# The end of the gate-row chain moved from VectorE to GpSimd and ScalarE, and its transposes six places later

## The chip, the cores and the metric

One core of a Trainium2 chip runs the whole kernel. Times are microseconds of device time for one execution; the figure for a kernel is the median of several runs. The engines are TensorE (PE in the profile), VectorE (DVE), ScalarE (ACT), GpSimd (POOL) and SyncE (SP). Each takes its own instructions in order and waits for the others by semaphores.

## The reference

Two decoder layers over 512 tokens of width 1024, in float32. Each layer projects its input once, runs two branches over four heads each, and merges them:

```python
p = x @ W_in                       # q|k|v|gate, mLSTM q|k|v|o|i|f, merge gates
y_A = P_A(swish(g) * HeadNorm(Retention(q, k, v)))
y_B = P_B(sigmoid(o) * HeadNorm(mLSTM(conv(q), conv(k), v, i, f)))
x = LN(alpha * x + W_out(sigmoid(gA) * y_A + sigmoid(gB) * y_B))
x = LN(alpha * x + SwiGLU(x))
```

The mLSTM branch needs, for each head, rows over the 512 tokens made from the two scalar gates i and f:

```python
log_f = log_sigmoid(f_pre)
b = cumsum(log_f)                  # in chunks
m = running maximum of (i - b)     # the stabiliser
# weights exp(...) of the scores and of the carried state use b, i - b and m
```

These rows are the gate-row chain. The change concerns its last three operations: -(b + m), a copy of that row to the place from which it is transposed, and -m.

## The kernel before, in words

**Tiles.** Every matrix product is done in three float32 matmuls: operands are split into a rounded high part and the rest, and high x high, high x low and low x high are summed in PSUM. Weights arrive in 512 KB tiles (`wraw`, SP's queue, five buffers); ScalarE casts the high part (`whi`, L201) and VectorE subtracts for the low part (`wlo`, `lo_of`, L133). This is done about four tiles ahead of the matmuls.

**Stages of a layer.** For each of two pairs of retention heads, p = 0 and 1: four feature blocks for q and k (L266 to L268), then a value block (`tok_units`, L357 to L359, four weight tiles times four token blocks of 128), then a gate block of the same form. After the first pair's q and k comes one block for the mLSTM's i and f (`feat_if`). Then follow the mLSTM heads, the merge, and the SwiGLU. A value block's four PSUM banks are evacuated by ScalarE (`rvh`, L714) and VectorE (`rvl`, L133); the gate block needs the same four banks.

**Order.** TensorE's and SP's instructions run in the order in which the code issues them. For the other engines a scheduler places the instructions of these stages; GpSimd, VectorE and ScalarE then run in that order.

**Places for side work.** `tok_units` and `feat_mms` call `slot()` after each group of matmuls. `slot()` takes one step of the first generator in the queue `side`: `scores` (3 steps; scores and weights of one head), `weighted` (5 steps; the state and four token blocks of weighted sums, L491 to L493), `head_norms`, `if_cols` (the transposes of the gate rows), and `rest(n)`, n steps that do nothing. A value or gate block has 16 places. After the gate block of each pair, `drain()` runs whatever is left in the queue, one step after another.

For p = 0 the queue at the value block is: `scores` of head 0, `rest(12)`, `if_cols`; behind it come `weighted` of head 0, `scores` of head 1, `rest(2)`, `weighted` of head 1.

**The gate-row chain.** `if_evac` (L632 on) makes the rows in the tile `rows`, four rows of heads in each of four slices r0 to r3, on VectorE and ScalarE, ending with a running maximum in two scans (L654). Its last three operations are at L658 to L660. Then r2 and the value `mp` are written to DRAM (`md`, L661 and L662, GpSimd's queue), from where they are read back over all partitions much later (`negm`, L740). `if_cols` transposes r3 on TensorE (L668), and copies the result to `cols` (L669) and `en` (L670), which the mLSTM stages use.

Of the kernel before, what the change touches and what calls it, by code (L numbers as in the profile page):

```python
# [13 lines left out]
ALU = mybir.AluOpType  # L14
# [90 lines left out]
def decoder_trunk(ctx: ExitStack, tc: tile.TileContext, wall, xT_in, x_in, pvec, lnp, rtab, out):  # L105
    nc = tc.nc
# [135 lines left out]
    side, slow = deque(), deque()  # L242
# [49 lines left out]
    def feat_split(xh, xl, evacs, between):  # L292

        ws = [take() for _ in evacs]
        pms = [main_bank() for _ in evacs]
        for n, (pm, w) in enumerate(zip(pms, ws)):
            feat_mms(pm, w, xh, xl, 0, S // 2, False)
            between(n)
        for pm, w, ev in zip(pms, ws, evacs):
            feat_mms(pm, w, xh, xl, S // 2, S)  # L300
            used()
            ev(pm)
# [277 lines left out]
    def input_sums(xh, xl, sh, sl):  # L580

        t1, t2 = slice(0, S // 2), slice(S // 2, S)
        for m in range(4):
            t = scratch([P, 2, S], "xs")
            for i in range(2):
                nc.gpsimd.tensor_tensor(out=t[:, i], in0=xh[:, m + 4 * i].bitcast(F32), in1=xl[:, m + 4 * i].bitcast(F32), op=ALU.add)
            yield
            f = scratch([P, 4, S // 2], "sf")
            a11, a12, a21, a22 = t[:, 0, t1], t[:, 1, t1], t[:, 0, t2], t[:, 1, t2]
            for i, a, b, op in ((0, a21, a22, ALU.subtract), (1, f[:, 0], a11, ALU.subtract),  # L590
                                (2, a11, a21, ALU.subtract), (3, f[:, 1], a12, ALU.add)):
                nc.vector.tensor_tensor(out=f[:, i], in0=a, in1=b, op=op)
            nc.scalar.copy(sh[:, :, m], f)
            lo_of(sl[:, :, m], f, sh[:, :, m])
            yield

    def rest(n):
        for _ in range(n):
            yield

    for l in range(L):
# [10 lines left out]
        def rot_evac(dst):  # L612
            def ev(pm):
                t = scratch([P, S], "rt")
                nc.vector.tensor_tensor(out=dst, in0=pm, in1=tab[:, 0], op=ALU.mult)
                nc.vector.tensor_tensor(out=t[0:64], in0=pm[64:128], in1=tab[0:64, 1], op=ALU.mult)
                nc.vector.tensor_tensor(out=t[64:128], in0=pm[0:64], in1=tab[64:128, 1], op=ALU.mult)
                nc.gpsimd.tensor_tensor(out=dst, in0=dst, in1=t, op=ALU.add)
            return ev
# [12 lines left out]
        def if_evac(pm):  # L632
            F = slice(32, 36)
            r0, r1, r2, r3 = (rows[:, i] for i in range(4))
            nc.gpsimd.memset(r3[0:32], 0.0)
            nc.vector.tensor_scalar(out=r0[0:36], in0=pm[0:36], scalar1=pv[0:36, C_BIF : C_BIF + 1], scalar2=None, op0=ALU.add)
            nc.vector.tensor_tensor(out=r0[0:36], in0=pm[64:100], in1=r0[0:36], op=ALU.add)
            nc.scalar.activation(r1[F], r0[F], AF.Abs)
            nc.scalar.activation(r1[F], r1[F], AF.Exp, scale=-1.0)
            nc.vector.tensor_scalar(out=r2[F], in0=r1[F], scalar1=1.0, scalar2=None, op0=ALU.add)  # L640
            nc.scalar.activation(r3[F], r2[F], AF.Ln)
            nc.vector.scalar_tensor_tensor(out=r1[F], in0=r2[F], scalar=-1.0, in1=r1[F], op0=ALU.add, op1=ALU.subtract)
            nc.scalar.activation(r2[F], r3[F], AF.Exp, scale=-1.0)
            nc.vector.tensor_tensor(out=r1[F], in0=r1[F], in1=r2[F], op=ALU.mult)
            nc.vector.tensor_tensor(out=r3[F], in0=r3[F], in1=r1[F], op=ALU.subtract)
            nc.vector.scalar_tensor_tensor(out=r1[F], in0=r0[F], scalar=0.0, in1=r3[F], op0=ALU.min, op1=ALU.subtract)
            for a in (slice(0, HC), slice(HC, S)):
                nc.vector.tensor_tensor_scan(out=r2[F, a], data0=r1[F, a], data1=r1[F, a], initial=0.0,
                                             op0=ALU.add, op1=ALU.min)
            nc.vector.tensor_copy(r1[0:4], r2[F])  # L650
            nc.vector.tensor_tensor(out=r3[0:4], in0=r0[0:4], in1=r1[0:4], op=ALU.subtract)
            mp = sm.tile([4, 1], F32, tag="mp", name="mp")
            for a, first in ((slice(0, HC), 0.0), (slice(HC, S), mp)):
                nc.vector.tensor_tensor_scan(out=r2[0:4, a], data0=r3[0:4, a], data1=r3[0:4, a], initial=first,  # L654
                                             op0=ALU.max, op1=ALU.max)
                if a.start == 0:
                    nc.vector.tensor_tensor(out=mp, in0=r1[0:4, HC - 1 : HC], in1=r2[0:4, HC - 1 : HC], op=ALU.add)
            nc.vector.scalar_tensor_tensor(out=r0[0:4], in0=r1[0:4], scalar=-1.0, in1=r2[0:4], op0=ALU.mult, op1=ALU.subtract)  # L658
            nc.vector.tensor_copy(r3[32:36], r0[0:4])
            nc.vector.tensor_scalar(out=r2[0:4], in0=r2[0:4], scalar1=-1.0, scalar2=None, op0=ALU.mult)  # L660
            nc.gpsimd.dma_start(md[:, :S], r2[0:4])  # L661
            nc.gpsimd.dma_start(md[:, S:], mp)  # L662

# [9 lines left out]
        for p in range(2):  # L673
            if p == 1:
                slow.append(input_sums(xh, xl, *xs))
            qk = reg.tile([P, 4, S], F32, tag="qk", name="rqk")
            rots = [rot_evac(qk[:, i]) for i in range(4)]
            if p == 0 and l > 0:
                feat_split(xh, xl, rots, between)
            elif p == 0:  # L680
                first_units(rots)
            else:
                for ev in rots:
                    feat(xh, xl, ev)
            if p == 0:
                feat_if(xh, xl, if_evac)
            boxes = [[None], [None]]

            def ret_weights(h):
                a = slice(h % 2 * HC, (h % 2 + 1) * HC)  # L690
                dec, qdec = tab[:, 2 + h // 2, a], tab[:, 4 + h // 2, a]

                def mult(o, a, c):
                    nc.vector.tensor_tensor(out=o[:, :HC], in0=a[:, :HC], in1=dec, op=ALU.mult)
                    nc.vector.tensor_tensor(out=o[:, HC:], in0=a[:, HC:W1], in1=dec[:, :P], op=ALU.mult)

                def key_weight():
                    return [pv[:, C_KW + 2 * h + j : C_KW + 2 * h + j + 1] for j in range(2)]

                def query_weight(o, q):  # L700
                    nc.vector.tensor_tensor(out=o, in0=q, in1=qdec, op=ALU.mult)

                return mult, key_weight, query_weight

            side.append(scores(qk, 0, boxes[0], *ret_weights(2 * p)))
            if p == 0:
                side.append(rest(12))
                side.append(if_cols())
            vh = reg.tile([P, NB, 2, DV], F32R, tag="vh", name="rvh")
            vl = reg.tile([P, NB, 2, DV], F32R, tag="vl", name="rvl")  # L710

            def v_evac(b, pm, vh=vh, vl=vl):
                src = pm.rearrange("p (h d) -> p h d", h=2)
                nc.scalar.copy(vh[:, b], src)  # L714
                lo_of(vl[:, b], src, vh[:, b])

            tok_units([main_bank() for _ in range(NB)], lambda k: xh[:, k], lambda k: xl[:, k], K8, True, True, v_evac)
            oo = reg.tile([P, 2, NB, DV], F32, tag="oo", name="roo")

            def o_done(hh, oo=oo):  # L720
                def done(i, pa):
                    nc.scalar.copy(oo[:, hh, i], pa[:, :DV])
                return done

            side.append(weighted(boxes[0], vh, vl, 0, DV, o_done(0)))
            side.append(scores(qk, 1, boxes[1], *ret_weights(2 * p + 1)))
            side.append(rest(2))
            side.append(weighted(boxes[1], vh, vl, 1, DV, o_done(1)))
            gt = reg.tile([P, NB, 2 * DV], F32, tag="gt", name="rgt")

            def g_evac(b, pm, gt=gt):
                nc.scalar.activation(gt[:, b], pm, AF.Silu)

            tok_units([main_bank() for _ in range(NB)], lambda k: xh[:, k], lambda k: xl[:, k], K8, True, True, g_evac)
            drain()
            gain = pv[:, C_RG : C_RG + 8]
            side.append(head_norms(oo, p, gt, gain, od[0]))
# [493 lines left out]
```

## Time and profile before

| | |
|---|---|
| median of 3 runs | 1776.57 us (1776.14 to 1777.71) |
| the profiled execution, its own time | 1777.92 us |
| its span, first to last instruction | 1776.2 us |
| granted TensorE clock, mean | 0.998 |
| TensorE busy | 1759.9 us, 99% |
| VectorE busy | 1312.9 us, 74% |
| ScalarE busy | 793.6 us, 45% |
| GpSimd busy | 433.3 us, 24% |
| the place of the change, layer 0 | 58 to 94 us |
| the place of the change, layer 1 | 937 to 973 us |

A row of a timeline has the start, the duration (both us), the engine, the line, the operation, what it writes and reads, the shape and the count; in brackets the idle time before it and what ended that. A row of waits has who waited for whom, the sum, the number and the longest. A row of groups has the number of instructions, busy us, the mean ns of one, and the idle time before.

### The profile page before, as it was taken

The page shows a single profiled execution, that of the slowest core. Times are in us where ns is not written, and L with a number is a line of the kernel's source. Part 1 is how long each engine was busy: PE and PEld are TensorE (multiplying, and loading weights), DVE is VectorE, ACT ScalarE, POOL GpSimd, SP SyncE. Part 2 cuts the span into 40 slices and gives each one's busy share as a digit, 9 for nine tenths or more (in the row PEclk, how much of TensorE's full clock was granted, in tenths as well). Part 3 has the DMA queues.
Part 4 walks back from the last instruction along what each step waited for, and adds up shares of the span by engine and source line. Part 5 has one row for each costly group of instructions (what it writes and reads, how often), then busy time and mean ns, then how long its engine had stood idle before and what let it go on. Part 6 is the DMA issues. An engine that isn't in the chain of part 4 may idle for free.

```text
span 1776.2 us, 27128 instructions
## 1 busy us (share of the span) xinstructions
PE 1759.9 (99%) x10904; PEld 1586.3 (89%) x10904; DVE 1312.9 (74%) x1726; ACT 793.6 (45%) x1148; POOL 433.3 (24%) x321
## 2 busy tenths in 40 slices
PE   9999999999999999999999999999999999999997
PEld 7888898998889999988898898989988899999886
DVE  6676878795559999963476968787845699998534
ACT  4445555663226444451244455556533254445310
POOL 2141110231001555520121311113300115555200
PEclk9999999999999999999999999999999999999999
DMA  7232422346333323363242323313553223333521
GB/s 250 86 105 72 143 72 96 106 137 239 96 111 110 105 96 108 107 213 95 83 166 89 110 88 106 119 60 108 200 180 119 95 95 108 111 116 114 186 69 48
DMA packets 74878, 209.48 MB, mean 118 GB/s; under 512 B 6616, under 2 KB 8536, under 8 KB 73728
## 3 DMA queue, kind: packets, MB, share of 16 engines
q1 hardware_dynamic: 64912, 168.32, 29.6%
q0 software_dynamic: 9840, 39.43, 6.3%
q8 instruction: 86, 1.41, 0.3%
q14 instruction: 40, 0.33, 0.1%
HBM read 190.93 MB, written 16.79 MB: 117 GB/s over the span
## 4 chain that ended last, share of the span: by engine, by line
PE 97%; DVE 1%; ACT 0%; issue 0%; DMA 0%; SPq 0%; DVEq 0%
PE pm L324 31%; PE pm L357 9%; PE pm L359 9%; PE pm L358 9%; PE pm L266 6%; PE pm L268 6%; PE pm L267 6%; PE pa L324 5%; PE pa L358 3%; PE pa L357 3%; PE pa L359 3%; PE pa L491 1%; PE pa L492 1%; PE pa L493 1%; PE pa L547 1%; PE pa L465 1%
## 5 line engine op out<-in xcount | busy, mean ns | idle before, releaser
L133 DVE TENSOR_TENSOR wlo<-wraw,whi 128x1024 fp32r<-128x1024 f32 (+2 forms) x416 | 599.6, 1453 | 203.1 <-ACT whi L201 200.5
L201 ACT CAST whi<-wraw 128x1024 fp32r<-128x1024 f32 x403 | 421.1, 1049 | 476.2 <-PE pm L267 116.0
L447 POOL TENSOR_TENSOR rs<-ve,nhalf 128x4 f32<-128x4 f32 (+1 forms) x32 | 33.0, 1033 | 480.2 <-DVE ve L446 480.2
L223 POOL TENSOR_TENSOR wraw<-wraw 128x1024 f32<-128x1024 f32 x32 | 77.0, 2405 | 150.9 <-issue 58.1
L357 PE MATMUL pm<-whi,x0h 128*128 128x512 f32 x256 | 102.5, 400 | 1.8 <-DVE rvl L133 1.7
L357 PE MATMUL pm<-whi,x20h 128*128 128x512 f32 x256 | 102.5, 400 | 0.6 <-DVE rvl L133 0.6
L359 PE MATMUL pm<-wlo,x0h 128*128 128x512 f32 x256 | 100.3, 392 | 0.0
L359 PE MATMUL pm<-wlo,x20h 128*128 128x512 f32 x256 | 100.3, 392 | 0.0
L358 PE MATMUL pm<-whi,x20l 128*128 128x512 f32 x256 | 100.1, 391 | 0.0
L358 PE MATMUL pm<-whi,x0l 128*128 128x512 f32 x256 | 100.1, 391 | 0.0
L1082 POOL TENSOR_TENSOR qa<-qa 128x512 f32<-128x512 f32 x20 | 42.8, 2142 | 142.3 <-DVE qa L1081 90.4
L324 PE MATMUL pm<-x10h,whi 128*128 128x256 f32 x240 | 67.9, 283 | 0.0
L324 PE MATMUL pm<-x10l,whi 128*128 128x256 f32 x240 | 67.9, 283 | 0.0
L324 PE MATMUL pm<-s0h,whi 128*128 128x256 f32 x240 | 67.9, 283 | 0.0
L324 PE MATMUL pm<-s0l,whi 128*128 128x256 f32 x240 | 67.9, 283 | 0.0
L324 PE MATMUL pm<-s0h,wlo 128*128 128x256 f32 x240 | 67.9, 283 | 0.0
L324 PE MATMUL pm<-x11h,whi 128*128 128x256 f32 x240 | 67.9, 283 | 0.0
L324 PE MATMUL pm<-x11l,whi 128*128 128x256 f32 x240 | 67.9, 283 | 0.0
L324 PE MATMUL pm<-x11h,wlo 128*128 128x256 f32 x240 | 67.9, 283 | 0.0
L324 PE MATMUL pm<-s1h,whi 128*128 128x256 f32 x240 | 67.9, 283 | 0.0
L324 PE MATMUL pm<-s1l,whi 128*128 128x256 f32 x240 | 67.9, 283 | 0.0
L324 PE MATMUL pm<-s1h,wlo 128*128 128x256 f32 x240 | 67.9, 283 | 0.0
(519 smaller groups left out, 5672.5 us busy)
## 6 DMA issues: line engine op xcount, KB each, us to landing
wraw<-wall SPq DMA_DIRECT2D x307, 512.0 KB, 3.8
od<-ot POOLq DMA_DIRECT2D x16, 512.0 KB, 3.6
of<-od POOLq DMA_DIRECT2D x16, 512.0 KB, 4.8
gb<-lnp POOLq DMA_DIRECT2D x4, 1024.0 KB, 6.3
x1d<-xr POOLq DMA_DIRECT2D x8, 512.0 KB, 3.0
xr<-x1d POOLq DMA_DIRECT2D x8, 512.0 KB, 4.6
negm<-md POOLq DMA_DIRECT2D x2, 1026.0 KB, 6.3
xr<-xtok POOLq DMA_DIRECT2D x4, 512.0 KB, 7.4
```

The costliest lines, as they stand in the source:

```text
L133: nc.vector.tensor_tensor(out=out_lo, in0=full, in1=hi.bitcast(F32), op=ALU.subtract)
L201: nc.scalar.copy(hi, sum_t[i])
L223: nc.gpsimd.tensor_tensor(out=raw_t[u + 2], in0=raw_t[u], in1=raw_t[u + 3], op=ALU.add)
L266: nc.tensor.matmul(pm[:, c0:c1], lhsT=hi[:, k], rhs=xh[:, k, c0:c1], start=(k == 0), stop=False)
L267: nc.tensor.matmul(pm[:, c0:c1], lhsT=hi[:, k], rhs=xl[:, k, c0:c1], start=False, stop=False)
L268: nc.tensor.matmul(pm[:, c0:c1], lhsT=lo[:, k], rhs=xh[:, k, c0:c1], start=False, stop=(k == KT - 1))
L324: nc.tensor.matmul(pm, lhsT=x[:, j, k], rhs=y[:, k], start=go and n == 0, stop=j == 1 and k == 3 and n == 2, skip_group_check=not first)
L357: nc.tensor.matmul(pm, lhsT=sh(k)[:, a], rhs=hi[:, j], start=first, stop=False)
L358: nc.tensor.matmul(pm, lhsT=sl(k)[:, a], rhs=hi[:, j], start=False, stop=False)
L359: nc.tensor.matmul(pm, lhsT=sh(k)[:, a], rhs=lo[:, j], start=False, stop=last)
L447: nc.gpsimd.tensor_tensor(out=rs[:, :n], in0=ve[:, :n], in1=nhalf[:, :n], op=ALU.pow)
L1082: nc.gpsimd.tensor_tensor(out=v, in0=v, in1=u, op=ALU.subtract)
```

## The change

The negation of r2 comes first, on GpSimd; -(b + m) is then r2 minus r1, on GpSimd; the copy to r3 is on ScalarE. `if_cols` stands behind 18 steps of rest instead of 12.

```diff
-            nc.vector.scalar_tensor_tensor(out=r0[0:4], in0=r1[0:4], scalar=-1.0, in1=r2[0:4], op0=ALU.mult, op1=ALU.subtract)
-            nc.vector.tensor_copy(r3[32:36], r0[0:4])
-            nc.vector.tensor_scalar(out=r2[0:4], in0=r2[0:4], scalar1=-1.0, scalar2=None, op0=ALU.mult)
+            nc.gpsimd.tensor_scalar(out=r2[0:4], in0=r2[0:4], scalar1=-1.0, scalar2=None, op0=ALU.mult)
+            nc.gpsimd.tensor_tensor(out=r0[0:4], in0=r2[0:4], in1=r1[0:4], op=ALU.subtract)
+            nc.scalar.copy(r3[32:36], r0[0:4])
             nc.gpsimd.dma_start(md[:, :S], r2[0:4])
             nc.gpsimd.dma_start(md[:, S:], mp)
...
             if p == 0:
-                side.append(rest(12))
+                side.append(rest(18))
                 side.append(if_cols())
```

What it moves, on the engines that wait or are waited for there. ScalarE, layer 0, at the end of the value block:

```order
 L201 CAST whi<-wraw 128x1024 x2
+L660 COPY rows<-rows 4x512
 L714 CAST rvh<-pm 128x512 x3
 L201 CAST whi<-wraw 128x1024
 L714 CAST rvh<-pm 128x512
```

The new copy stands behind both weight casts and ahead of the evacuation of the value block. In layer 1, at the same place:

```order
-L201 CAST whi<-wraw 128x1024 x2
+L201 CAST whi<-wraw 128x1024
+L660 COPY rows<-rows 4x512
+L201 CAST whi<-wraw 128x1024
 L714 CAST rvh<-pm 128x512 x3
 L201 CAST whi<-wraw 128x1024
 L714 CAST rvh<-pm 128x512
```

Here it stands ahead of the second weight cast too. VectorE, layer 0 (layer 1 has the same rows):

```order
 L657 TENSOR_TENSOR mp<-rows 4x1
 L654 SCALAR_TENSOR_TENSOR rows<-rows,mp 4x256
-L658 SCALAR_TENSOR_TENSOR rows<-rows 4x512
-L659 COPY rows<-rows 4x512
-L660 TENSOR_SCALAR rows<-rows 4x512
 L133 TENSOR_TENSOR wlo<-wraw,whi 128x1024
 L133 TENSOR_TENSOR rvl<-pm,rvh 128x512 x3
```

After the second scan the weight's low part and the value block's low parts come at once. GpSimd, layer 0, between the rotation of q and k and the head norms:

```order
 L618 TENSOR_TENSOR rqk<-rqk,rt 128x512 x4
 L662 DMA md<-mp 4x1
+L658 TENSOR_SCALAR rows<-rows 4x512
+L659 TENSOR_TENSOR rows<-rows 4x512
 L661 DMA md<-rows 4x512
 L447 TENSOR_TENSOR rs<-ve,nhalf 128x4
```

Both new operations stand between the two DMA issues. On TensorE the four transposes (L668) stand six groups of gate matmuls later, and at the end of the gate block of p = 0 (the last rows before the next feature block, L266, in layer 0):

```order
 L493 MATMUL pa<-pp 128x256
-L357 MATMUL pm<-whi,x0h 128x512
-L358 MATMUL pm<-whi,x0l 128x512
-L359 MATMUL pm<-wlo,x0h 128x512
-L357 MATMUL pm<-whi,x0h 128x512
-L358 MATMUL pm<-whi,x0l 128x512
-L359 MATMUL pm<-wlo,x0h 128x512
+L491 MATMUL pa<-rvh,pp 128x256
+L492 MATMUL pa<-rvl,pp 128x256
+L493 MATMUL pa<-rvh,pp 128x256
```

The last matmuls there are now those of `weighted`, where gate matmuls stood before.

## The prediction

> **What bounds the kernel now.** I read the head of the page, the chain of work that ended last, and then the waits of TensorE.
>
> ```profile
> PE 1759.9 (99%) x10904; PEld 1586.3 (89%) x10904; DVE 1312.9 (74%) x1726; ACT 793.6 (45%) x1148; POOL 433.3 (24%) x321
> PE 97%; DVE 1%; ACT 0%; issue 0%; DMA 0%; SPq 0%; DVEq 0%
> PE pm L357 <- DVE rvl L133: 2.3, 2, 1.7
> PE pa L668 <- DVE rows L659: 0.2, 1, 0.2
> ```
>
> TensorE is the bound from end to end. So a change on the other engines can gain no more than the TensorE waits it touches. Those are the last two rows: the first matmul of the retention gate block waits for the evacuation of the value block (2.3 us over both layers, 1.7 at most), and the gate-row transposes wait 0.2 us. The ceiling of any gain is 2.5 us, or 0.14%. A loss has no such ceiling. I count a difference under 0.2% (3.6 us) as one that a measurement of this kernel cannot tell from none.
>
> Next I read the timelines of the place, by engine. Layer 0 (ScalarE, VectorE, GpSimd, TensorE):
>
> ```profile
> 54.25 1.05 ACT L201 CAST whi<-wraw 128x1024 fp32r<-128x1024 f32 x1 [3.22 <-PE pm L358]
> 55.84 0.59 ACT L714 CAST rvh<-pm 128x512 fp32r<-128x512 f32 x1 [0.53 <-PE pm L359]
> 58.13 0.74 DVE L654 TENSOR_TENSOR_SCAN rows<-rows,mp 4x256 f32<-4x256 f32 x1
> 58.91 0.68 DVE L658 SCALAR_TENSOR_TENSOR rows<-rows 4x512 f32<-4x512 f32 x1
> ...
> 60.41 1.21 DVE L133 TENSOR_TENSOR wlo<-wraw,whi 128x1024 fp32r<-128x1024 f32 x1
> 61.55 1.87 DVE L133 TENSOR_TENSOR rvl<-pm,rvh 128x512 fp32r<-128x512 f32 x3
> 58.39 0.53 POOL L662 DMA_DIRECT2D md<-mp  x1 [17.18 <-DVE mp L657]
> 60.77 0.54 POOL L661 DMA_DIRECT2D md<-rows  x1 [1.85 <-DVE rows L660]
> 59.49 0.39 PE L359 MATMUL pm<-wlo,x0h 128*128 128x512 f32 x1
> 60.09 0.44 PE L668 MATMUL pa<-ident,rows 36*128 36x36 f32 x4 [0.21 <-DVE rows L659]
> 62.27 0.50 PE L357 MATMUL pm<-whi,x0h 128*128 128x512 f32 x1 [1.74 <-DVE rvl L133]
> ```
>
> ScalarE makes the first rvh at 55.84, long before VectorE comes to its rvl at 61.55, because VectorE is busy with the gate rows. The gate block starts 0.72 after rvl does. In layer 1:
>
> ```profile
> 935.03 1.06 ACT L201 CAST whi<-wraw 128x1024 fp32r<-128x1024 f32 x1 [3.48 <-PE pm L358]
> 937.47 0.74 DVE L654 TENSOR_TENSOR_SCAN rows<-rows,mp 4x256 f32<-4x256 f32 x1
> ...
> 939.74 1.21 DVE L133 TENSOR_TENSOR wlo<-wraw,whi 128x1024 fp32r<-128x1024 f32 x1
> 940.88 1.87 DVE L133 TENSOR_TENSOR rvl<-pm,rvh 128x512 fp32r<-128x512 f32 x3
> 937.72 0.53 POOL L662 DMA_DIRECT2D md<-mp  x1 [18.39 <-DVE mp L657]
> 941.60 0.50 PE L357 MATMUL pm<-whi,x20h 128*128 128x512 f32 x1 [0.58 <-DVE rvl L133]
> ```
>
> **The change, part by part.** *Removed from VectorE:* the three operations from 58.91 to 60.41, 1.5 us a layer. By themselves they would let wlo and rvl start 1.5 us earlier.
>
> *Added on ScalarE, and where it stands.* The new copy of the gate row waits for GpSimd. In ScalarE's order it stands ahead of the three rvh casts in layer 0. In layer 1 it stands ahead of the weight cast whi and the three rvh. ScalarE takes its work in order, so casts that were done from 55.84 on now wait for a chain that cannot begin before L654 ends, at 58.87. This turns the saving into a loss; it is the main term.
>
> *Prices.* No row shows a GpSimd tensor_scalar, or a subtraction on 4 partitions. The nearest rows (by line and form; for L618 the least, median and largest of its 16, with their first and last start), and a ScalarE operation on 4x512:
>
> ```profile
> L635 POOL MEMSET rows<- 32x512 f32 x2 | 1.1, 536 | 1.5 <-PE pm L359 1.5
> L800 POOL TENSOR_SCALAR_AFFINE_SELECT pf<-pf 128x128 f32<-128x128 f32 x32 | 11.4, 387 | 67.6 <-ACT pf L798 63.7 <-issue 3.9
> L618 POOL TENSOR_TENSOR rqk<-rqk,rt x16: 1287/2314/2336, 28.0 to 998.7; 128x512 f32<-128x512 f32 x16
> L771 POOL TENSOR_TENSOR mu<-mu 128x512 f32<-128x512 f32 x4 | 5.2, 1293 | 54.1 <-DVE mu L770 54.1
> 41.81 0.63 ACT L638 ACTIVATE rows<-rows 4x512 f32<-4x512 f32 x1 [4.53 <-DVE rows L637]
> ```
>
> The negation lies between the memset of as many columns (0.54) and four of L800's 128 columns (4 x 0.39 = 1.55). I take 0.75, since it is nearer to the memset in size and adds one read. The subtraction costs 1.29 (L771) to 2.34 (L618's most); I take 1.30, since VectorE, which runs two-input operations beside L618, will mostly stand idle here. With 0.05 between them GpSimd's part is 2.1 us (1.9 to 3.9). The ScalarE copy is 0.63.
>
> A rule of the Trainium skill bears on the price that has no row. GPSIMD Engine Reference, section Engine selection, calls a one-input GpSimd operation roughly line-rate and a two-input one about twice as slow as VectorE. L771 agrees for the second (1.29 against 0.68 for L658); no row here shows the first. As an estimate by that page the negation would cost about what the memset does, and the whole change 0.4 us less.
>
> *Layer 0.* GpSimd is free at 58.92 (the L662 issue ends) and starts at 58.95. Its part ends at 61.05, and the copy runs from 61.08 to 61.71. The first rvh (0.59) ends at 62.30 and rvl starts at 62.33. The gate block starts 0.72 later, at 63.05 instead of 62.27: +0.8. The wlo of 60.41 moves to 58.9, and its whi of 54.25 is still ahead of the copy, so it is not late.
>
> *Layer 1.* GpSimd starts at 938.28 and ends at 940.38; the copy ends at 941.04. Then comes the whi that stood at 935.03. Its wlo, which stands ahead of rvl on VectorE, can start 1.09 after whi does (the pair 93.27 and 94.36 below): 942.13. rvl follows 1.14 later (60.41 to 61.55), at 943.27, and the gate block 0.72 after that, at 943.99 instead of 941.60: +2.4.
>
> *The transposes, six places later.* Where they stood they ran inside the stall and cost nothing. Among gate matmuls they take TensorE time, at most the 0.44 of their row; I take 0.25 a layer: +0.5. Their rows are ready at 61.7, and six places of 1.4 us after 63 is 71, so they no longer wait.
>
> *What the six places push out.* There are 32 places for side work in the value and gate blocks (16 each). It used 31: 3 for scores, 12 of rest, 1 for transposes, 5 + 3 + 2 + 5 for the heads. With 18 of rest it needs 37, so the last five, the weighted sums of head 1, run back to back after the last gate matmul, with no gate matmuls between to hide their evacuation. The rows of that end in layer 0, ScalarE, VectorE, and the TensorE cadence:
>
> ```profile
> 93.27 1.05 ACT L201 CAST whi<-wraw 128x1024 fp32r<-128x1024 f32 x1 [0.33 <-PE pm L358]
> 94.23 0.59 ACT L732 ACTIVATE rgt<-pm 128x512 f32<-128x512 f32 x1
> 83.66 0.37 ACT L504 CAST pp<-pa 128x256 fp32r<-128x256 f32 x1 [1.71 <-PE pa L493]
> 94.36 1.23 DVE L133 TENSOR_TENSOR wlo<-wraw,whi 128x1024 fp32r<-128x1024 f32 x1 [0.53 <-ACT whi L201]
> 84.06 0.42 DVE L133 TENSOR_TENSOR pp<-pa,pp 128x256 fp32r<-128x256 f32 x1 [1.73 <-ACT pp L504]
> 63.77 0.28 PE L491 MATMUL pa<-rvh,pp 128*128 128x256 f32 x1
> 64.48 0.40 PE L357 MATMUL pm<-whi,x0h 128*128 128x512 f32 x1
> ```
>
> Six of these matmuls take 0.71, so 0.12 each. From the end T of the gate block, 18 run before the first that reads the state (6 + 3 + 6 + 3): T + 2.1. The state's high part (L504) stands behind whi and the last rgt on ScalarE. With T at 93.1 those start at T + 0.2 and T + 1.1, so L504 would end near T + 2.1. The low part comes behind wlo on VectorE (T + 1.3 + 1.14) and ends near T + 2.9; ScalarE enters late, having the other rgt and the moved copies ahead, by up to half a microsecond. The stall is 0.8 (0.3 to 1.5) a layer: +1.6.
>
> *DMAs and queues.* The two issues of md stay on GpSimd; the second leaves about 0.3 us later than at 60.77. Its first reader is issued at 156.41 (below), so this costs nothing. The weight casts held on ScalarE are for units about three ahead, 5.4 us each; 4 us of delay are covered by that. SP's loads keep their order.
>
> ```profile
> 156.41 0.61 POOL L740 DMA_DIRECT2D negm<-md  x1 [2.96 <-DVE qf L701]
> ```
>
> *Sum:* 0.8 + 2.4 + 0.5 + 1.6 = +5.3 us. The profiled execution took 1777.92 us by its own time (1.7 around its span of 1776.2); the median shown is 1776.57, 1.35 less. The sum is a difference and goes on the median: 1781.9 us, 0.30% slower. Lower end: GpSimd 1.9, transposes 0.3 in all, drains 0.3 each give 0.6 + 2.2 + 0.3 + 0.6 = +3.7. Upper end: GpSimd 3.9, transposes 0.9, drains 1.5 each give 2.6 + 4.2 + 0.9 + 3.0 = +10.7.
>
> **The rivals.** *The clock falls in the stalls.* TensorE would now stand still from about 59.7 to 63.05 and from 940.5 to 944.0, 3.4 us each; before it was 2.5 in layer 0, with four transposes inside. What a longer stop does is seen at the start:
>
> ```profile
> 12.16 0.49 PE L344 MATMUL pm<-x0h,whi 128*128 128x512 f32 x1 [1.91 <-ACT whi L430]
> 13.00:13.50 0.50, 0.05 (x1) 0.06 (x1) 0.50 (x3) 0.37 (x1) 0.00 (x0) 0.50 1.12 315
> 58.00:64.00 6.00, 4.05 (x21) 3.02 (x20) 5.87 (x11) 2.33 (x4) 1.07 (x2) 1.00 0.34 104
> ```
>
> TensorE idles from 10.25 to 13.45 with one matmul at 12.16, and the granted clock (the third number from the right) is 0.50 at 13.0; it is back to full near 16.3. Over the 2.5 us stop at 60 it stayed 1.00. At half clock for some 3.2 us the loss is about 1.6 us a stop, 1.6 to 3.2 in all: 1783.5 to 1785.1. Against it: the stop is barely longer than the one at the start. The Trainium skill's TensorE: Matmul & The Clock Gate, section Why this matters for your kernels, asks for no idle gaps over about 3 us; by that page both stops would fall to half clock, as an estimate +3.2, and the row at 13.0 agrees that a stop of that size can.
>
> *Not slower beyond measurement.* The end of the gate block hides the drain, because the high and low state are made before T + 2.1. This needs ScalarE to reach L504 about 0.8 us earlier than the rows say. The two stalls alone give 3.2 + 0.5 = +3.7, or +2.8 + 0.3 = 3.1 with GpSimd at its low end: 1779.7 to 1780.3, where the 0.2% line is 1780.1. The mechanism decides when the drain costs under 0.1 a layer and GpSimd under 2.0 us. For it: VectorE is relieved. Against it: whi and rgt stand ahead of L504.
>
> *The copy does not hold ScalarE up.* If GpSimd needed only 0.4 us, layer 0 would gain 0.9 and layer 1 lose 0.7, and with 0.5 and 1.6 the sum would be +1.9, 1778.5. If the hold did not exist at all, the 2.5 us ceiling less 0.5 and 1.6 leaves about -0.4: 1776.2. The order of ScalarE's work speaks against it, and every GpSimd price above is over 1.8.
>
> **How the numbers follow.** Chances: the sum as worked out, with the clock held, 0.47; the clock falling at one stop or both, 0.30; not slower beyond measurement, 0.17; no hold, 0.06. The first is the likeliest: 1781.9. The range goes down into the third case, 1779.5, and up to the second with its larger stalls, 1786.5. Slower by over 0.2%: 0.47 + 0.30 and a little of the third, 0.79. Within: 0.18. Faster: 0.03, since a gain over 0.2% would exceed the ceiling of 2.5 us.
>
> **What would show it.** In the profile after, the wait of L357 for rvl should be about 3.3 us in layer 0 and 3.5 in layer 1, and on ScalarE the copy on L660 should start near 61.1 and 940.4 with the rvh casts behind it. A new TensorE wait on L491 or L492 for the state, 0.5 to 1 us, should stand after the last gate matmul of each layer, and L668 should not wait. The granted clock just after both stops tells the first rival. The prediction is wrong if GpSimd's two operations take under 1.5 us or over 4 together, if L357's waits stay near 2 us, or if TensorE waits at a place not named here.

## The result, and the profile after

The changed kernel takes 1791.69 us (median of six runs, 1790.32 to 1793.98), the kernel before 1777.14 beside it (1776.14 to 1780.74). The ratio is 1.0075, with a 95% interval of 1.0065 to 1.0085: 0.75% slower, some 14 us, where 5.3 us and at most 1786.5 us were forecast. The sign was right and the size was not. The kernel before took 1776.1 to 1776.7 us in runs with a mean granted clock of 0.999 and 1780.0 to 1781.0 in runs with 0.996 (among the 27 beside e5 to e8), so a difference of 1 or 2 us between two medians says little and the rows decide; one run of 9110.24 us, beside e1 to e4, counts in no ratio. The profiled execution took 1791.62 us with a span of 1789.9, so 13.7 us stand between the two spans; that is what the rows have to account for.

First the same lines of the page and of TensorE's waits (who waited for whom, the sum in us, the number, the longest):

```profile
PE 1765.5 (99%) x10904; PEld 1588.6 (89%) x10904; DVE 1308.0 (73%) x1720; ACT 792.9 (44%) x1150; POOL 443.4 (25%) x325
PE pm L357 <- DVE rvl L133: 9.0, 2, 4.8
PE pa L492 <- DVE pp L133: 0.9, 2, 0.5
PE pa L491 <- ACT pp L504: 0.8, 2, 0.4
```

The gate block's first matmul waits 9.0 us instead of 2.3. Two waits are new, on the state in the drain. L668 is gone from the list. The waits add up to 8.2 us more, and 13.7 are missing. The rest is counted as busy time, which rose by 5.6 us for the same 10904 instructions: the matmuls ran, or followed one another, more slowly.

The stop in layer 0, by engine (GpSimd, ScalarE, VectorE, TensorE):

```profile
58.92 2.38 POOL L658 TENSOR_SCALAR rows<-rows 4x512 f32<-4x512 f32 x1
61.39 1.25 POOL L659 TENSOR_TENSOR rows<-rows 4x512 f32<-4x512 f32 x1
62.67 0.62 ACT L660 COPY rows<-rows 4x512 f32<-4x512 f32 x1 [7.40 <-POOL rows L659]
63.31 1.56 ACT L714 CAST rvh<-pm 128x512 fp32r<-128x512 f32 x3
58.76 1.19 DVE L133 TENSOR_TENSOR wlo<-wraw,whi 128x1024 fp32r<-128x1024 f32 x1
63.93 1.29 DVE L133 TENSOR_TENSOR rvl<-pm,rvh 128x512 fp32r<-128x512 f32 x2 [3.99 <-ACT rvh L714]
64.67 0.80 PE L357 MATMUL pm<-whi,x0h 128*128 128x512 f32 x1 [4.83 <-DVE rvl L133]
```

This is the chain that the prediction drew: GpSimd, the copy, the rvh casts behind it, rvl, the gate block. ScalarE stands still for 7.40 us with the rvh casts queued behind its copy. In layer 1 the weight cast and its split lie in between, as forecast:

```profile
944.66 1.50 POOL L658 TENSOR_SCALAR rows<-rows 4x512 f32<-4x512 f32 x1
946.24 1.27 POOL L659 TENSOR_TENSOR rows<-rows 4x512 f32<-4x512 f32 x1
947.54 0.62 ACT L660 COPY rows<-rows 4x512 f32<-4x512 f32 x1 [9.64 <-POOL rows L659]
949.26 1.23 DVE L133 TENSOR_TENSOR wlo<-wraw,whi 128x1024 fp32r<-128x1024 f32 x1 [4.70 <-ACT whi L201]
951.14 0.50 PE L357 MATMUL pm<-whi,x20h 128*128 128x512 f32 x1 [4.13 <-DVE rvl L133]
```

Then the windows behind the two stops (the granted clock is the third number from the right):

```profile
65.00:66.00 1.00, 1.00 (x3) 0.81 (x3) 0.97 (x3) 1.00 (x2) 0.00 (x0) 0.50 0.00 0
68.00:70.00 2.00, 2.00 (x10) 1.65 (x9) 0.00 (x0) 0.00 (x0) 0.00 (x0) 1.00 0.76 240
953.00:955.00 2.00, 2.00 (x6) 1.56 (x5) 1.02 (x2) 0.00 (x0) 0.00 (x0) 0.50 0.51 104
```

The clock fell to half after both stops. Last the end of the gate block in layer 0, with what stood beside it (VectorE, GpSimd, TensorE):

```profile
88.34 2.08 DVE L133 TENSOR_TENSOR wlo<-wraw,whi 128x1024 fp32r<-128x1024 f32 x1
90.34 1.64 DVE L133 TENSOR_TENSOR pp<-pf,pp 128x384 fp32r<-128x384 f32 x1
88.06 3.51 POOL L586 TENSOR_TENSOR xs<-x0h,x0l 128x512 f32<-128x512 f32 x2
93.70 0.39 PE L359 MATMUL pm<-wlo,x0h 128*128 128x512 f32 x1
97.42 0.38 PE L491 MATMUL pa<-pp 128*128 128x256 f32 x1 [0.37 <-ACT pp L504]
98.25 0.38 PE L492 MATMUL pa<-pp 128*128 128x256 f32 x1 [0.45 <-DVE pp L133]
99.66 0.40 PE L266 MATMUL pm<-x0h,whi 128*128 128x512 f32 x1
```

The tail from the last gate matmul to the next block is 99.66 - 93.70 = 5.96 us. Thirty matmuls at 0.12 and the gate matmul's own 0.22 make 3.8; so 2.1 are stall. (Start to start, TensorE's rhythm was 0.23 at full clock; the durations shown overlap.)

From the end of the value block to the next block, layer 0 took 6.4 us more than before and layer 1 7.3. They split so:

| term, us | layer 0 | layer 1 | sum | forecast |
|---|---|---|---|---|
| gate block starts later | 2.4 | 3.2 | 5.6 | 3.2 |
| half clock behind the stop | 1.3 | 1.6 | 2.9 | 0 (rival: 1.6 to 3.2) |
| drain | 2.1 | 2.1 | 4.2 | 1.6 |
| transposes | 0.5 | 0.5 | 1.0 | 0.5 |
| sum | 6.3 | 7.4 | 13.7 | 5.3 |

The half clock is counted by start times: in layer 0 the first ten gate matmuls took 3.53 us where before they took 2.19, the six of `weighted` among them left out. The transposes' part is what they add to the rhythm around them.

### The profile page after: what moved, and what is told of

It reads as the page before. It is cut to its first block, busy times and chain, and to the rows that moved or that the text cites. A ratio compares the mean times of both kernels' runs of the same rounds, so it can differ in the third digit from the quotient of the medians.

```text
span 1789.9 us, 27124 instructions
## 1 busy us (share of the span) xinstructions
PE 1765.5 (99%) x10904; PEld 1588.6 (89%) x10904; DVE 1308.0 (73%) x1720; ACT 792.9 (44%) x1150; POOL 443.4 (25%) x325
## 4 chain that ended last, share of the span: by engine, by line
PE 93%; DVE 3%; ACT 2%; issue 1%; DMA 0%; POOL 0%; SPq 0%; DVEq 0%; ACTq 0%
PE pm L324 31%; PE pm L357 9%; PE pm L359 9%; PE pm L358 9%; PE pm L266 5%; PE pm L268 5%; PE pm L267 5%; PE pa L324 5%; PE pa L357 3%; PE pa L358 3%; PE pa L359 3%; PE pa L492 1%; PE pa L491 1%; PE pa L493 1%; DVE wlo L133 1%
## 5 line engine op out<-in xcount | busy, mean ns | idle before, releaser
L447 POOL TENSOR_TENSOR rs<-ve,nhalf 128x4 f32<-128x4 f32 (+1 forms) x32 | 33.3, 1042 | 494.5 <-DVE ve L446 494.5
L324 PE MATMUL pm<-x10h,wlo 128*128 128x256 f32 x240 | 67.9, 283 | 0.0
```

Of the source, the lines that this page charges most:

```text
L324: nc.tensor.matmul(pm, lhsT=x[:, j, k], rhs=y[:, k], start=go and n == 0, stop=j == 1 and k == 3 and n == 2, skip_group_check=not first)
L447: nc.gpsimd.tensor_tensor(out=rs[:, :n], in0=ve[:, :n], in1=nhalf[:, :n], op=ALU.pow)
```

## The experiments

The theory after the result (A in the expectations): the hold of ScalarE, the half clock that follows from it, and the drain make the whole loss. The first four runs undo or cover parts of these, two put a version together, three take the drain apart, and one measures the price. Ratios are to the kernel before on the same chip: 1778.03 us beside e1 to e4, 1778.06 beside e5 to e8, 1778.25 beside e9 and e10.

**Engines without the places (e1).** The changed kernel, with the transposes back at their place.

```diff
-                side.append(rest(18))
+                side.append(rest(12))
```

> The three operations on GpSimd and ScalarE, the transposes where they were (12 steps of rest). Theory A (the ScalarE copy holds the value block's evacuation behind GpSimd, 2.4 + 3.2 us; the clock falls in both stops, about 3.0; the last five side steps lose their cover, 4.2; the transposes cost 0.9): only the first two are left, so about 8.5 us over before, 1785.5, with waits of L357 or L668 of 4 to 5 us and a granted clock of 0.5 behind them. Theory B (the loss comes from the six places, and the move of engines is hidden but for its effect on the clock): at most 2 us over before, 1779.

1787.3 us, ratio 1.0054 (1.0040 to 1.0068). Over A's 1785.5, far over B's. By the rows the gate block starts as late as in the changed kernel (5.6 us over both layers) and the drain and the transposes, 5.2 us, are gone. But the half clock now costs 5.0 us instead of 2.9; in layer 0 it is still at 0.50 from 68 to 70 us. Why it lasts longer is not shown. TensorE's waits:

```profile
PE pa L668 <- ACT rows L660: 4.7, 2, 3.5
PE pm L357 <- DVE rvl L133: 3.4, 2, 2.5
```

**Places without the engines (e2).** The kernel before, with only the transposes later.

```diff
-                side.append(rest(12))
+                side.append(rest(18))
```

> The chain stays on VectorE; only the transposes stand six places later (18 steps of rest). Theory A: the drained weighted sums cost about 4.2 over both layers and the transposes up to 0.9; L668's wait of 0.2 goes; 1781.5 to 1782.5, with the clock at 1.00 throughout and L357's wait as before (1.7 to 2.4 in layer 0). Theory B: about 12 us over before, 1789.

1783.59 us, ratio 1.0036 (1.0023 to 1.0049), 1 to 2 over the forecast. What was not forecast is the clock: the stop in layer 0, as long as before (2.79 us from start to start, 2.78 before), now ended at half clock, with the four transposes no longer in it. The last matmul ahead of the stop, the first behind it, and a window of this kernel:

```profile
59.94 0.39 PE L359 MATMUL pm<-wlo,x0h 128*128 128x512 f32 x1
62.73 0.79 PE L357 MATMUL pm<-whi,x0h 128*128 128x512 f32 x1 [2.40 <-DVE rvl L133]
64.00:66.00 2.00, 2.00 (x6) 1.52 (x6) 1.61 (x2) 0.00 (x0) 0.00 (x0) 0.50 0.45 182
```

So moving the transposes alone went with half clock in one stop. That they had kept the clock up is not shown: e8 below has the same stop with them in it, and it fell too. In the longer stops of e1 they did not keep the clock either.

**The stop filled (e3).** The changed kernel, with 18 matmuls of 128x512 ahead of the gate block, whose result nobody reads. They do not shorten the hold; they keep TensorE at work in it.

```diff
+            [nc.tensor.matmul(f, lhsT=xh[:, i % KT, :P], rhs=xl[:, i % KT], start=True, stop=True) for f in ([aux_bank()] if p == 0 else []) for i in range(18)]
```

> The whole change, and 18 matmuls of 128x512 that nothing reads (about 4.1 us a layer) ahead of the retention gate block of the first pair, where TensorE would stand idle. Theory A: they fit into the stops (4.8 and 4.1 us), the clock stays at 1.00 and the 3.0 us of half clock are gone: about 1788.7, the copy and the gate block starting when they did. If the clock did not matter (the matmuls after the stop are slow for another reason, such as late operands), the time stays 1791.7 or rises.

1788.85 us, ratio 1.0064 (1.0051 to 1.0077). That is 2.8 less than the changed kernel, but the two intervals overlap, so the rows must decide. The windows behind the stops are at full clock:

```profile
64.00:68.00 4.00, 3.47 (x15) 2.88 (x16) 3.49 (x5) 2.16 (x4) 0.00 (x0) 1.00 0.08 10
951.00:955.00 4.00, 4.00 (x20) 3.30 (x19) 1.51 (x2) 0.00 (x0) 0.00 (x0) 1.00 0.60 210
```

The gate block starts as late as in the changed kernel, and its first ten matmuls take 2.18 us in both layers. From the end of the value block to the next block it is 1.3 and 1.6 us shorter: this prices the half clock at 2.9 us, as the account has it.

**The copy behind the casts (e4).** The changed kernel, with ScalarE's copy issued in `if_cols` and given a zero bias that is made from the last rvh, so that it stands behind all four rvh casts. A tiny ScalarE operation (0.20) is added.

```diff
-            nc.scalar.copy(r3[32:36], r0[0:4])
...
+            nc.scalar.activation(r3[32:36], rows[0:4, 0], AF.Identity, bias=late0[0:4, 0:1])
...
+                nc.scalar.activation(late0[0:4], vh[0:4, b, 0, 0:1].bitcast(F32), AF.Copy, scale=0.0)
```

> The whole change, but the ScalarE copy of the gate row takes a bias (a zero made from the last rvh), which puts it behind the value block's evacuation in ScalarE's order; all else in the same order. Theory A: nothing is held, the stops go, and with them the clock's fall: the gate block starts some 1.6 us earlier than before in layer 0 and 1.0 in layer 1; the drain (4.2) and the transposes (0.9) stay: about 2.5 us over before, 1779.6. Rival C (GpSimd's operations slow VectorE's wlo and rvl beside them, and that is what makes the stop): the stop stays at 2 us or more a layer, 1784 or above.

1780.46 us, ratio 1.0015 (1.0006 to 1.0024). A holds. GpSimd does the same work, and in its profile the negation is even slower in layer 1 (2.38 in both layers); but some 11 us are gone, with the hold, the half clock and most of the wait that was there before. The copy and TensorE's waits:

```profile
62.93 0.73 ACT L665 ACTIVATE rows<-rows,late 4x512 f32<-4x512 f32 x1 [2.65 <-POOL rows L659]
PE pm L357 <- DVE rvl L133: 0.8, 1, 0.8
PE pa L492 <- DVE pp L133: 0.9, 2, 0.5
PE pa L491 <- ACT pp L504: 0.8, 2, 0.4
```

What is left over the kernel before, 2.4 us with an interval of 1.1 to 4.3, holds the drain and the transposes, less what the gate block gains. It starts 1.16 and 0.23 us after the last value matmul instead of 2.78 and 1.33, so 4.2 + 1.0 - 2.7 = 2.5. ScalarE's place in the order made the stops; GpSimd's time only sets how long they are.

**No drain (e5).** The same, with GpSimd adding r1 and r2 first, the sign turned in ScalarE's copy, the negation of r2 last, and 13 steps of rest, so that the 32 places just suffice.

```diff
+            nc.gpsimd.tensor_tensor(out=r0[0:4], in0=r2[0:4], in1=r1[0:4], op=ALU.add)
+            nc.gpsimd.tensor_scalar(out=r2[0:4], in0=r2[0:4], scalar1=-1.0, scalar2=None, op0=ALU.mult)
...
+            nc.scalar.activation(r3[32:36], rows[0:4, 0], AF.Identity, scale=-1.0, bias=late0[0:4, 0:1])
...
+                side.append(rest(13))
```

> The changed kernel with three edits: GpSimd first adds r1 and r2, ScalarE's copy turns the sign and stands behind the rvh casts, the negation of r2 comes last, and rest is 13, so that all 32 places are used and nothing is left for the drain. Theory A (the whole loss is the hold of ScalarE with the half clock behind it, plus the drain, plus the transposes): against the kernel before, TensorE's waits fall by about 1.7 us (2.5 to 0.8) and the transposes cost 0.5 to 0.9, so 1777.2 us where the kernel before is 1778.0 (1776.0 to 1778.5), no wait on L491 or L492. Theory B (GpSimd and ScalarE in this work cost TensorE something by themselves): 1780 or more with the drain gone.

1777.19 us, ratio 0.9991 (0.9982 to 1.0000). A's number. GpSimd and ScalarE can do this work at no cost that these runs can tell. One wait is new, the transposes for the copy in layer 1:

```profile
PE pa L668 <- ACT rows L665: 1.1, 1, 1.1
PE pm L357 <- DVE rvl L133: 0.8, 1, 0.8
```

**One place later (e10).** The run before, with the rests 14 and 1, to take that wait away.

```diff
-                side.append(rest(13))
+                side.append(rest(14))
...
-            side.append(rest(2))
+            side.append(rest(1 if p == 0 else 2))
```

> e5_no_drain with rest 14 ahead of the transposes and 1 ahead of head 1's sums: the transposes stand one place later, still with 32 places used. In layer 1 they waited 1.1 us for the copy; one place is 1.4 us, so that wait goes. Theory A: 1776.2 us where e5_no_drain is 1777.2 and the kernel before 1778.0. Theory B (a later place brings head 0's sums too late for something else, or one rest less makes head 1's sums wait): 1777 or more with a new TensorE wait in the list.

1777.63 us, ratio 0.9993 (0.9984 to 1.0002). The wait went, but the time did not follow, and the rows say why. TensorE's list of waits has no new entry, yet the matmuls of head 1's state now stand apart; GpSimd, VectorE and TensorE in layer 0:

```profile
77.67 3.51 POOL L586 TENSOR_TENSOR xs<-x0h,x0l 128x512 f32<-128x512 f32 x2
77.95 2.08 DVE L133 TENSOR_TENSOR wlo<-wraw,whi 128x1024 fp32r<-128x1024 f32 x1
83.92 0.39 PE L493 MATMUL pa<-rvh,pp 128*128 128x256 f32 x1
```

L492 started at 83.67 and the next matmul after this L493 at 84.32, where 0.12 is the rhythm; these gaps make about 0.6 us in each layer. One place was enough to bring GpSimd's input sums beside VectorE's splits, as in the drain of the changed kernel (e9 below); in e5 the weight split came behind them and took 1.21. So B's second guess came true in a small form. From the end of the value block to the next block, layer 0 takes 0.55 us more than in e5 and layer 1 0.47 less. Neither version can be told from the kernel before.

**The drain by itself (e6).** The kernel before, with 8 steps of rest ahead of head 1's sums of the first pair.

```diff
-            side.append(rest(2))
+            side.append(rest(8 if p == 0 else 2))
```

> The kernel before, with only the rest ahead of head 1's weighted sums made 8 for the first pair, so that these five steps run after the gate block, with head 1's scores long done and the first input sums on GpSimd long over. The tail from the last gate matmul to the next block took 5.96 us in the changed kernel. Theory A (the prediction's stall of 0.8 a layer was right for a drain by itself, and the rest came from GpSimd's sums beside VectorE and from key weights made late): tail 4.6 us, +1.6 us in all, 1779.6. Theory B (the tail itself stalls by 2.1): tail near 6.0, +4.2, 1782.2.

1777.3 us, ratio 0.9996 (0.9987 to 1.0004): no loss that can be told, less than either theory. The last gate matmul, the state's wait and the next block:

```profile
89.48 0.40 PE L359 MATMUL pm<-wlo,x0h 128*128 128x512 f32 x1
92.37 0.39 PE L492 MATMUL pa<-pp 128*128 128x256 f32 x1 [0.20 <-DVE pp L133]
93.80 0.39 PE L266 MATMUL pm<-x0h,whi 128*128 128x512 f32 x1
```

The tail is 4.32 us, with 0.5 of stall. From the end of the value block to the next block the layers take 0.34 and 0.32 us more than before, 0.7 in all, which the interval of the time (-2.3 to +0.7 us) allows. The state's evacuation, on which the prediction put its 0.8, costs little. Most of the 2.1 came from elsewhere.

**The drain with late scores (e7).** The kernel before, with six of the steps of rest ahead of head 1's scores, which then stand right before the drain.

```diff
-            side.append(scores(qk, 1, boxes[1], *ret_weights(2 * p + 1)))
+            side.append(rest(6 if p == 0 else 0)); side.append(scores(qk, 1, boxes[1], *ret_weights(2 * p + 1)))
```

> As the run before, but with the six empty places ahead of head 1's scores, so that these stand right before the drain as in the changed kernel, while GpSimd's first input sums stay early. If the key weights made late are what lengthens the tail: about 5.9 us, +4 in all, 1782. If it is GpSimd's sums beside VectorE: the tail is that of the run before.

1777.56 us, ratio 0.9999 (0.9991 to 1.0008), tails of 4.29 and 4.31 us. Late scores do not lengthen the tail by themselves.

**The sums early (e9).** The changed kernel, with GpSimd's input sums (L586) begun one pair earlier.

```diff
-            if p == 1:
+            if p == 0:
                 slow.append(input_sums(xh, xl, *xs))
```

> The changed kernel with the second half's input sums (GpSimd, L586) begun one pair earlier. In layer 1 none of them is left near the drain; in layer 0 one pair still stands behind L447 there. Theory A (GpSimd's sums slow VectorE's weight split and score split and so make the key weights late): layer 1's tail from the last gate matmul to the next block falls from 5.95 us to 4.3 to 4.6, with wlo at 1.23 instead of 2.08 and pp at 0.55 instead of 1.64 there, while layer 0's stays near 5.9. Theory B (head 0's later norms and the order of the queue lengthen the tail): 5.9 in both. Only the two tails are read; sums that now fall into the stops may lengthen these.

The whole kernel took 1802.19 us in its one run, 10.5 more than the changed kernel: among other things, one of the sums now stands between the negation and the subtraction in layer 0, at 62.14, and the stop there grows to 6.45 us. Only the two tails are read. Layer 0, which still has a pair of sums there, keeps a tail of 5.93 us and a wlo of 2.15; in layer 1, without them (VectorE, then TensorE):

```profile
987.02 1.21 DVE L133 TENSOR_TENSOR wlo<-wraw,whi 128x1024 fp32r<-128x1024 f32 x1
988.15 0.55 DVE L133 TENSOR_TENSOR pp<-pf,pp 128x384 fp32r<-128x384 f32 x1
992.43 0.40 PE L359 MATMUL pm<-wlo,x20h 128*128 128x512 f32 x1
995.32 0.38 PE L492 MATMUL pa<-pp 128*128 128x256 f32 x1 [0.19 <-DVE pp L133]
996.72 0.40 PE L266 MATMUL pm<-x20h,whi 128*128 128x512 f32 x1
```

The tail is 4.29 us. So A: both splits have their old length, and 1.66 of the 2.1 us of stall are gone. The stop is short in this layer too, 0.73 us, but that is not the reason: e4 has no stops and keeps tails of 5.95 and 5.97. The chain is this: with the transposes six places later, head 0's sums come later, and with them L447, for which GpSimd waits; the input sums stand behind it in GpSimd's queue and slide from 75.5 to 88.1, onto VectorE's splits of the key weights, just ahead of the drain.

**GpSimd's prices (e8).** The kernel before, with 24 more GpSimd operations a layer on unused rows (written out below; the run has them in one line). They ran at the start of each layer, from 5.5 and 896.9 us on. The time was 1786.28 us, one run.

```diff
+            nc.gpsimd.memset(rows[64:68], 1.0)
+            for i in range(6):
+                for n in (S, P):
+                    x = rows[64:68, i % 3, :n]
+                    nc.gpsimd.tensor_scalar(out=x, in0=x, scalar1=-1.0, scalar2=None, op0=ALU.mult)
+                    nc.gpsimd.tensor_tensor(out=x, in0=x, in1=x, op=ALU.mult)
```

> The kernel before with 24 more GpSimd operations a layer behind the md issues, on unused rows: tensor_scalar by -1 and tensor_tensor product, in turns, on 4x512 and 4x128, six of each. Theory A (the negation's price is the operation's own, and VectorE's two-input work beside it lengthens it): tensor_scalar on 4x512 about 1.5 us in idle stretches of VectorE and up to 2.4 beside it, tensor_tensor 1.25 and up to 2.6; on 128 columns about a quarter to a third. Theory B (2.38 and 1.50 were the cost of a first use): later ones near the 0.75 of the prediction. The time is higher where GpSimd's later work is put off, and says nothing else.

The groups by form (busy us, mean ns), and a stretch in which VectorE is idle:

```profile
L663 POOL TENSOR_SCALAR rows<-rows 4x512 f32<-4x512 f32 x12 | 20.4, 1701 | 1.0
L663 POOL TENSOR_TENSOR rows<-rows 4x512 f32<-4x512 f32 x12 | 14.0, 1176 | 0.5
L663 POOL TENSOR_SCALAR rows<-rows 4x128 f32<-4x128 f32 x12 | 8.6, 720 | 1.0
...
904.30 1.48 POOL L663 TENSOR_SCALAR rows<-rows 4x512 f32<-4x512 f32 x1
906.05 0.69 DVE L615 TENSOR_TENSOR rqk<-pm,rtab 128x512 f32<-128x512 f32 x1 [4.28 <-PE pm L268]
```

A for the negation: it costs 1.5 us with VectorE idle (the last row's 4.28 us of idle time cover it), as in layer 1 of the changed kernel, and 1.7 in the mean of twelve. It is no cost of a first use. The two-input product took 1.18 in the mean. One pair ran at 1.1 each beside VectorE, which this does not explain; spans on GpSimd are rough. On 128 columns the negation took 0.72, which is 0.42 of the time on 512 and more than A's quarter to a third; as an estimate from these two means, some 0.4 us of it is fixed.

The same trace bears on the clock. The stop of layer 0 has the transposes in it, as in the kernel before, and the same wait for rvl:

```profile
59.49 0.44 PE L668 MATMUL pa<-ident,rows 36*128 36x36 f32 x4
61.67 0.50 PE L357 MATMUL pm<-whi,x0h 128*128 128x512 f32 x1 [1.74 <-DVE rvl L133]
63.00:64.00 1.00, 1.00 (x4) 0.73 (x3) 1.00 (x2) 0.22 (x1) 0.00 (x0) 0.50 0.82 328
```

The clock fell to half behind it. From start to start this stop is 2.59 us; at 2.78 it kept full clock in the kernel before, e6 and e7, and at 2.79 it fell in e2. What decides is not shown.

## Why the prediction was wrong in size

*Right:* the bound, the ceiling, the sign, and the order on ScalarE as the main term. The negation by itself accounts for the misses at the copy: 62.67 instead of 61.08, since it took 2.38 instead of 0.75. The subtraction (1.25 and 1.27 for 1.30), the copy (0.62 for 0.63), the cast of layer 1 in between, and the md issues and weight casts that cost nothing came as the prediction had them. L668 does not wait. The measured 13.7 us by the rows are 8.4 over the forecast: 2.4 from the negation, 2.9 from the clock, 2.6 from the drain and the rest from the transposes.

*Price of the negation, 0.75 with bounds 0.54 to 1.55.* This step failed. It measured 2.38 in layer 0 and 1.50 in layer 1, and took the stops from the forecast 3.2 us to 5.6. The rows taken as nearest, a memset and a select, were no measure of an arithmetic operation. VectorE had done the same negation, in the kernel before, in about a quarter of the 1.50:

```profile
60.07 0.41 DVE L660 TENSOR_SCALAR rows<-rows 4x512 f32<-4x512 f32 x1
```

The Trainium skill's GPSIMD Engine Reference, section Engine selection, calls a one-input GpSimd operation roughly line-rate and a two-input one about twice as slow as VectorE. The two-input price agrees (1.25 for the subtraction, 0.68 for VectorE's L658). The one-input price does not: 1.50 against 0.41, and the measurement decides.

*The clock left out of the sum.* This step failed too. The rival was given 0.30 and its size, 1.6 to 3.2, held: 2.9 us. The prediction read the 2.5 us stop of the kernel before, which kept full clock, as a sign for longer ones. But that was one execution: the same stop fell in e2 and e8. What a stop of the forecast 3.4 us would have done, no trace shows. The prediction also counted against the fall that its stops were barely longer than the one at the start, though that one had ended at 0.50. Nor were the terms independent: the stops follow from the negation's price. The upper end of the sum, +10.7, and the clock's 3.2 were never added; together they are 13.9, close to the 13.7 measured. The Trainium skill's TensorE: Matmul & The Clock Gate, section Why this matters for your kernels, asks for no idle gaps over about 3 us. The trace of e2 fell after less: from 59.94 and one step of 0.23 to 62.73 are 2.6 us.

*The drain, 0.8 a layer.* The step named the state's evacuation behind whi and wlo. This step failed as well: 2.1 a layer was measured. Alone the evacuation costs 0.5 in a tail of 4.3 us. The other 1.66 a layer came from a queue that the prediction did not follow: GpSimd's, in which a later L447 carried the input sums onto VectorE's splits. The prediction counted the queues that the moved step passes, but not the work that moves with the places.

*Transposes, 0.25 a layer.* They cost about 0.5, just over the 0.44 that the prediction called the most.

## What to carry to other kernels

A small operation given to another engine is priced by what stands behind it in that engine's queue, and the stop it makes is priced again by the clock. One trace in which a stop keeps full clock does not show that the next execution will. When places in an order shift, follow every queue whose work is tied to them, for two operations that were apart before may now run side by side. An operation that no row shows is taken at least at its upper bound in a chain that ends on the bound engine: here even that bound, 1.55 us, was under the 2.38 of layer 0.

## What the runs showed of the hardware

- GpSimd's one-input tensor_scalar on 4x512 took 1.5 us with VectorE idle and 1.1 to 3.1 beside its work (e8, and e5 in layer 0); the two-input operations took 1.2 to 1.3 in the changed kernel, and up to 2.6 (e4, layer 0).
- GpSimd's two-input sums and VectorE's two-input splits from SBUF slow each other: VectorE's wlo took 2.08 us instead of 1.21 and pp 1.64 instead of 0.55 (the changed kernel and e9), and the pair of sums 3.51 instead of 2.86 (the kernel before). The Trainium skill's Advanced Engine Details and Errata, section GPSIMD Details, says that the two share a read and a write interface and conflict where VectorE has two SBUF inputs; these rows agree.
- Stops of TensorE ahead of this gate block, from the start of the last matmul to the next 128x512 one: at 4.5 to 6.5 us the granted clock fell to half each time (the changed kernel, e1, e9), at 2.6 to 2.8 us in two of five traces (e2, e8; not in the kernel before, e6, e7), at 1.3 us or less never.
